# Four outputs instead of three in token halves behind each layer norm, one PSUM bank each

## The chip, the core and the metric

The kernel runs on one core of one Trainium2 chip, as one program that is launched once. The metric is the device time of that launch in microseconds (us); smaller is better. TensorE multiplies into PSUM, which has eight banks of 128 partitions and 512 fp32 values each; VectorE, ScalarE (ACT in the rows) and GpSimd (POOL) do the rest from SBUF, and SyncE (SP) issues the DMAs. In the rows PE stands for TensorE and DVE for VectorE.

## What is computed

One sequence of 512 tokens with 1024 features goes through two blocks, all in fp32. The first block has two layers, the second one:

```python
def first_block(x, c, ...):
    c_act = silu(c)
    for l in range(2):
        sh1, sc1, g1, sh2, sc2, g2 = split(c_act @ w_ada[l] + b_ada[l], 6)
        h = x * (1 + sc1) + sh1
        if l == 0:
            y = short_conv_mixer(h, ...)          # W_out(B * conv3(C * V))
        else:
            h_kv = x * (1 + kv_scale) + kv_shift  # shift and scale from c, too
            k, v = h_kv @ w_k, h_kv @ w_v         # 16 heads of 64
            F = cumsum(log_sigmoid(h_kv @ w_f + b_f))
            # causal softmax of q.k / 8 + F[t] - F[s], times v, times w_o
            y = forgetting_attention(h, w_q, k, v, F, w_o)
        x = layer_norm(alpha * x + g1 * y, ln1[l])
        h = x * (1 + sc2) + sh2
        y = (silu(h @ w_gate[l]) * (h @ w_up[l])) @ w_down[l]     # 2816 wide
        x = layer_norm(alpha * x + g2 * y, ln2[l])
    return x

def second_block(x, p, ...):
    z = rms_norm(x) @ w_in                        # 256+256+64+5*512 outputs
    a = mla(...)                                  # latent attention, 4 heads
    r = hgrn2(...)                                # gated linear attention, both directions
    x = x + concat(a, r) @ w_o
    x = x + swiglu(rms_norm(x))
    return x + sigmoid(rms_norm(x) @ w_ple_gate) * (p @ w_ple_proj)
```

## The kernel before

Activations lie transposed: 128 features on the partitions, the 512 tokens on the free axis, so a tensor of 1024 features is eight tiles. Each operand of a product is split into an upper part (names that end in h, `whi` for weights) and the remainder (l, `wlo`), and `mm3` adds upper by upper, upper by remainder and remainder by upper into the same PSUM bank. One output tile over 1024 features therefore takes 8 x 3 matmuls.

**Weights** are packed in units of eight blocks of 128 x 128, in the order in which the program asks for them. `_make_unit` loads a unit by DMA into one of three slots (raw), casts it on ACT (whi) and subtracts on VectorE, sometimes on GpSimd (wlo); there are four slots for whi and four for wlo. `weight` makes units up to one beyond the unit that is asked for. The raw slots are shared with the **adaptive modulation** (w_ada): `ada_pump` takes a column of it at a time and multiplies and sums it on VectorE (aj, ada).

**Order.** The code is recorded first. `plan` then lists every engine's instructions with a cost model, by the order in the program and by what each needs: tiles, SBUF slots and PSUM banks in three classes (g, s, o; at most 6, 5 and 4 of the eight). `issue` emits this list, so nearly all instructions have one source line, L573, and are told apart here by the names of their tiles.

**The four junctions.** After a layer norm the first outputs of the next product are made in two token halves of 256 columns: TensorE multiplies the A half of all eight tiles while VectorE still normalizes the B half. `out_halves` gives a half a bank of its own, A of class g and B of class s, so three outputs take six banks; each half is read out for itself. This happens at four places:

- first FFN, behind the convolution's layer norm (tiles hm0 to hm7): gate 0, up 0 and gate 1 (pg0, pu0, pg1) in halves, in `ffn`; up 1 (pu) follows at full width, then gate 2 (pg, called pg2 below);
- attention, behind the first FFN's layer norm (tiles hk): the forget gates (pf) and the first two key outputs (pk0, pk1) in `fox_block`; then the forget gates' path (zf, the cumulative sum F, a trip of F through memory, the probabilities Pa, Pm, Pb), keys, values (pv: two banks, each holding two tiles of 128 tokens for two outputs, in `fox_v`) and queries (pq, from tiles hq);
- second FFN, behind the attention's layer norm, through `ffn` again;
- second block, behind the second FFN's layer norm (tiles hx): three of the five latent outputs (cq0 to cq2) in `block2`; cq3 and cq4 and the gates (gt) follow at full width. Here the norm's factor (rx, rxr) comes last and is multiplied into the outputs; ACT copies the halves to SBUF (cl) before it is known.

`gemm` runs a group of outputs: half by half, in a half tile by tile, in a tile output by output. In the first FFN `ffn` calls `ada_pump` for three columns per feature f, starting at f = 0. At the end of the layer norm's B half, `ln_mid` scales the eight tiles of x for the residual (agln, abln).

## Time and profile before

| what | value |
|---|---|
| median of three runs | 1951.23 us (1949.99 to 1951.87) |
| the profiled execution's own time | 1948.55 us |
| its span, first to last instruction | 1946.8 us |
| mean granted TensorE clock | 0.989 |
| TensorE busy | 1897.0 us (97%) |
| VectorE busy | 1285.9 us (66%) |
| ACT, GpSimd busy | 819.9 us (42%), 191.5 us (10%) |
| chain that ended last | TensorE 84%, VectorE 11% |

The times in the profile are of that one execution, from the start of its span. A matmul's duration in a timeline includes its pipeline; how fast matmuls follow each other is read from their starts. "[1.29 <-ACT hm0h L573]" says that the engine stood still for 1.29 us ahead of this instruction, and that ACT's writing of hm0h ended that.

### The profile page before, as it was taken

How to read it: one execution, taken by the hardware profiler on the slowest of the kernel's cores; microseconds unless marked ns; L12 is line 12 of the kernel's file. 1: busy time of each engine (PE TensorE's matmuls, PEld its weight loads, DVE VectorE, ACT ScalarE, POOL GpSimd, SP SyncE). 2: the span in 40 equal slices, each digit the busy share in tenths (PEclk: the TensorE clock that was granted, in tenths of full speed). 3: DMA queues.
4: the chain of work that ended last, by engine and by line, in shares of the span. 5: the costliest groups of instructions: out<-in, count | busy, mean ns of one | idle time of the engine just before them, and what ended most of it. 6: DMA issues, size and time to landing. Idle time of an engine off the chain costs nothing.

```text
span 1946.8 us, 24436 instructions
## 1 busy us (share of the span) xinstructions
PE 1897.0 (97%) x9310; PEld 1589.9 (82%) x9310; DVE 1285.9 (66%) x2211; ACT 819.9 (42%) x1363; POOL 191.5 (10%) x150
## 2 busy tenths in 40 slices
PE   8999899999999899999999999999999999999998
PEld 7888788888888788888888888787877888888887
DVE  8877976564569898894523335999898654334445
ACT  5323432222346577553322233686684533223333
POOL 1000100000001322110000000122153000000000
PEclk9999999999999899999999999999998999999999
DMA  9674477674424222323322222322111222222242
GB/s 360 223 249 158 138 248 241 199 236 161 150 98 138 70 76 88 120 76 109 103 98 98 98 97 76 130 87 76 55 55 44 97 98 97 95 96 94 97 139 75
DMA packets 76470, 245.55 MB, mean 126 GB/s; under 512 B 8496, under 2 KB 9776, under 8 KB 76352
## 3 DMA queue, kind: packets, MB, share of 16 engines
q1 hardware_dynamic: 76352, 243.98, 37.7%
q8 instruction: 73, 1.20, 0.2%
q14 instruction: 45, 0.37, 0.1%
HBM read 235.53 MB, written 8.42 MB: 125 GB/s over the span
## 4 chain that ended last, share of the span: by engine, by line
PE 84%; DVE 11%; ACT 2%; issue 2%; DMA 1%; SPq 0%; DVEq 0%; ACTq 0%
PE pu L573 18%; PE pg L573 17%; PE pd L573 12%; PE ffn_down L573 5%; PE gt L573 4%; PE wo L573 2%; PE pl L573 2%; PE gb L573 2%; PE gc L573 2%; PE vv L573 2%; PE attn_o L573 1%; PE pq L573 1%; PE conv_out L573 1%; DVE wlo L573 1%; PE pv L573 1%
## 5 line engine op out<-in xcount | busy, mean ns | idle before, releaser
L573 ACT CAST whi<-raw 128x1024 fp32r<-128x1024 f32 (+1 forms) x313 | 326.2, 1043 | 625.9 <-PE pd L573 130.8
L573 DVE TENSOR_TENSOR wlo<-raw,whi 128x1024 fp32r<-128x1024 f32 (+1 forms) x286 | 353.5, 1237 | 324.4 <-ACT whi L573 320.6
L573 POOL TENSOR_TENSOR wlo<-raw,whi 128x1024 fp32r<-128x1024 f32 x27 | 65.6, 2429 | 1181.7 <-ACT whi L573 1181.7
L573 DVE CUSTOM_DVE_ANT_0 aj<-ada,cact,adab 128x1024 bf16<-128x1024 f32 x96 | 123.8, 1293 | 37.7 <-DMA ada<-in_wada 37.5
L573 DVE TENSOR_TENSOR s<-pu,s 128x512 f32<-128x512 f32 x42 | 29.0, 690 | 85.0 <-PE pu L573 85.0
L573 DVE TENSOR_TENSOR S<-S,sq 128x512 f32<-128x512 f32 (+1 forms) x62 | 36.7, 592 | 1.6 <-ACT sq L573 1.4
L573 ACT ACTIVATE s<-s 128x512 f32<-128x512 f32 x22 | 13.9, 632 | 54.0 <-DVE s L573 54.0
L573 ACT ACTIVATE s<-pg 128x512 f32<-128x512 f32 x40 | 23.6, 589 | 18.3 <-PE pg L573 18.3
L573 DVE CUSTOM_DVE_ANT_0 G<-S,G 128x128 f32<-128x128 f32 (+3 forms) x64 | 30.3, 484 | 0.5
L573 DVE TENSOR_TENSOR xr<-pd,xr 128x512 f32<-128x512 f32 x16 | 11.0, 690 | 26.9 <-PE pd L573 26.9
L573 DVE TENSOR_SCALAR G<-Fm,fneg 128x128 f32<-128x128 f32 x64 | 26.6, 419 | 0.4 <-PE po L573 0.2
L573 POOL TENSOR_TENSOR Fm<-Fb,cmask 128x512 f32<-128x512 f32 x14 | 18.6, 1336 | 63.9 <-DVE PT_2l L573 30.3
L573 ACT ACTIVATE sq<-axr 128x256 f32<-128x256 f32 (+1 forms) x33 | 15.1, 467 | 22.0 <-DVE axr L573 22.0
L573 DVE TENSOR_SCALAR G<-Fb,fneg 128x128 f32<-128x128 f32 (+2 forms) x48 | 23.0, 480 | 0.4 <-PE po L573 0.2
L573 DVE TENSOR_TENSOR s<-pg,rfr 128x512 f32<-128x512 f32 x22 | 15.2, 691 | 11.9 <-PE pg L573 11.9
L573 DVE TENSOR_TENSOR u<-pu,rfr 128x512 f32<-128x512 f32 x22 | 15.2, 691 | 11.7 <-PE pu L573 11.7
L573 PE MATMUL tp<-ident,Pa 128*128 128x128 f32 x64 | 16.7, 289 | 3.8 <-DVE Pa L573 3.8
L573 ACT ACTIVATE Pa<-G,negm 128x128 f32<-128x128 f32 (+1 forms) x32 | 16.2, 506 | 9.8 <-DVE negm L573 8.8
L573 ACT ACTIVATE sq<-x 128x256 f32<-128x256 f32 (+1 forms) x19 | 9.8, 517 | 22.2 <-DVE x L573 22.2
L573 PE MATMUL tp<-ident,Pb 128*128 128x128 f32 x64 | 16.8, 293 | 2.0 <-DVE Pb L573 1.9
L573 DVE TENSOR_TENSOR gz<-gt,rxr 128x512 f32<-128x512 f32 x20 | 13.6, 685 | 4.7 <-PE gt L573 4.7
L573 PE MATMUL pu<-hm2l,whi 128*128 128x512 f32 x42 | 16.4, 390 | 0.0
(4502 smaller groups left out, 6314.9 us busy)
## 6 DMA issues: line engine op xcount, KB each, us to landing
raw<-in_wpack SPq DMA_DIRECT2D x309, 512.0 KB, 3.5
ada<-in_wada SPq DMA_DIRECT2D x96, 512.0 KB, 4.2
ada<-in_wada SPq DMA_DIRECT2D x32, 256.0 KB, 6.0
Fb<-fd SPq DMA_DIRECT2D x16, 256.0 KB, 3.8
x<-in_xT SPq DMA_DIRECT2D x8, 256.0 KB, 6.0
pd<-pple SPq DMA_DIRECT2D x8, 256.0 KB, 6.2
xd<-x SPq DMA_DIRECT2D x8, 256.0 KB, 6.2
axr<-xd SPq DMA_DIRECT2D x8, 256.0 KB, 4.5
```

Of the source, the lines that this page charges most:

```text
L573: getattr(getattr(nc, op.unit), op.name)(*[get(x) for x in op.args], **{k: get(x) for k, x in op.kw.items()})
```

## The change

Class `Wide` keeps both halves of an output in one bank: the A half's sum is made in columns 0 to 255 and the B half's in 256 to 511, and the whole bank is read out once, behind the B half (`full`). `gemm_wide` runs such a group, and for its length sets `ahead` to 1, so that `weight` makes no unit ahead of the one asked for.

- In both FFNs four outputs run in halves (pg0, pu0, pg1, pu1), on four banks, and `ada_pump` isn't called for the first two features.
- In the attention the forget gates and two keys take three banks, and the first values are multiplied beside them (`values`, `fox_v_part`): per tile the values of the half's tokens come with the last key. The eight narrow copies of the forget gates' weights are made ahead of the group.
- In the second block cq0 to cq3 run in halves; they are multiplied by the norm's factor straight out of PSUM, and the ACT copies go.

```diff
--- before.py
+++ after.py
@@ -30,6 +30,8 @@
 B2_ORDER = """gate1 proj0 gate0 score0 prep0 proj1 score1 gate2 intra0 value0 value1 proj2 gate3 state0 gout0
 prep1 score2 intra1 state1 prep2 intra2 proj3 score3 value2 prep3 state2 gout1 intra3 state3
 gout3 value3 gout2"""
+EARLY = 4
+LATE = 4
 MIX_GROUPS = [(0, 1, 2), (3,), (4,), (5,), (6,), (7,)]
 SLOTS = 76
 RAWB = 3
@@ -576,13 +578,21 @@
             nc.scalar.preload_act_table_set(load_at[i])
 
 
+class Wide(list):
+
+
+    def __init__(self, ps):
+        super().__init__([(ps[:, :HT], slice(0, HT)), (ps[:, HT:], slice(HT, T))])
+        self.full = [(ps, slice(0, T))]
+
+
 class Build:
     def __init__(self, ctx, tc, aps):
         self.tc = tc
         self.nc = Recorder()
         self.a = aps
         self.blocks = []
-        self.n_units = 0
+        self.n_units, self.ahead = 0, 2
         self.unit = {}
         self.ada_next = 0
         self.ada_jobs = []
@@ -632,7 +642,7 @@
         i = len(self.blocks)
         self.blocks.append((wname, k, n))
         u, s = divmod(i, BLK)
-        while self.n_units < min(u + 2, NUNIT):
+        while self.n_units < min(u + self.ahead, NUNIT):
             self._make_unit(self.n_units)
             self.n_units += 1
         hi, lo = self.unit[u]
@@ -667,7 +677,10 @@
         return [(self.ps("g", name + "A")[:, :HT], slice(0, HT)),
                 (self.ps("s", name + "B")[:, :HT], slice(HT, T))]
 
-    def gemm(self, outs, acts, kouter=True):
+    def out_wide(self, name, tag="g"):
+        return Wide(self.ps(tag, name))
+
+    def gemm(self, outs, acts, kouter=True, also=None):
 
 
         nc = self.nc
@@ -679,8 +692,10 @@
             for i, o in order:
                 wname, n, pieces = o
                 k, xh, xl = acts[i]
+                if also is not None and o is outs[-1]:
+                    also(p, i, xh, xl)
                 if (i, n, wname) not in ws:
-                    ws[i, n, wname] = (self.side_by_side if wname == "w_f" else self.weight)(wname, k, n)
+                    ws[i, n, wname] = self.narrow[:, k, :] if wname == "w_f" else self.weight(wname, k, n)
                 ps, sl = pieces[p]
                 if wname == "w_f":
                     for j, x in enumerate((xh, xl)):
@@ -694,15 +709,19 @@
 
         nc = self.nc
         hi, lo = self.weight(wname, k, n)
-        if k == 0:
-            self.narrow = self.r("narrow", (P, ND, 64))
         t = self.narrow[:, k, :]
         nc.scalar.copy(t[:, :32], hi[:, :32])
         nc.scalar.copy(t[:, 32:], lo[:, 32:64])
         return t
 
-    def gemm_all(self, outs, acts, kouter=True):
-        for _ in self.gemm(outs, acts, kouter):
+    def gemm_wide(self, outs, acts, also=None):
+
+        self.ahead = 1
+        self.gemm_all(outs, acts, also=also)
+        self.ahead = 2
+
+    def gemm_all(self, outs, acts, kouter=True, also=None):
+        for _ in self.gemm(outs, acts, kouter, also):
             pass
 
 
@@ -1090,9 +1109,10 @@
         wg, wu, wd = names
         early = []
         if halves:
-            early = [(wg, 0, self.out_halves("pg0")), (wu, 0, self.out_halves("pu0")),
-                     (wg, 1, self.out_halves("pg1"))]
-            self.gemm_all(early, acts)
+            early = [(w, f, self.out_wide(f"p{w[4]}{f}", tag)) for f, tag in enumerate("gs"[:EARLY // 2])
+                     for w in (wg, wu)]
+            self.gemm_wide(early, acts)
+            early = [(w, f, o.full) for w, f, o in early]
         else:
             early = [(wg, 0, self.out("pg0")), (wu, 0, self.out("pu0")), (wg, 1, self.out("pg1"))]
             self.gemm_all(early, acts)
@@ -1110,7 +1130,8 @@
                     pc.append(made[w, f])
 
                 left = (len(self.ada_jobs) - (ND if wg == "ffn_gate0" else 0)) - self.ada_next
-                self.ada_pump(min(left, 3 if wg == "ffn_gate0" else 1))
+                if f >= len(early) // 2:
+                    self.ada_pump(min(left, 3 if wg == "ffn_gate0" else 1))
                 s = self.f(f"s{f}")
                 if rstd is None:
                     for ps, sl in pc[0]:
@@ -1213,8 +1234,20 @@
     def fox_block(self, kva, qa, rest, ln):
         nc = self.nc
         nc.group = "fox"
-        pf, *pk = (self.out_halves(n) for n in ("pf", "pk0", "pk1"))
-        self.gemm_all([("w_f", 0, pf), ("w_k", 0, pk[0]), ("w_k", 1, pk[1])], kva)
+        pf, *pk = (self.out_wide(n) for n in ("pf", "pk0", "pk1"))
+        pv = self.fox_v_banks(0, "s")
+        ws = {}
+
+        def values(p, i, xh, xl):
+            if p == 0:
+                ws[i] = self.weights("w_v", i, 0, VP)
+            self.fox_v_part(pv, p, i, xh, xl, ws[i])
+
+        self.narrow = self.r("narrow", (P, ND, 64))
+        for k in range(ND):
+            self.side_by_side("w_f", k, 0)
+        self.gemm_wide([("w_f", 0, pf), ("w_k", 0, pk[0]), ("w_k", 1, pk[1])], kva, also=values)
+        pf, *pk = (x.full for x in (pf, *pk))
         nc.group = "rest"
         rest()
         nc.group = "logf"
@@ -1236,7 +1269,7 @@
         nc.sync.dma_start(fd.all(), F)
 
         ks = [self.fox_k(f, kva, pk[f]) for f in range(2)]
-        vs = self.fox_v(0, kva)
+        vs = self.fox_v(0, kva, pv)
         q = [self.fox_q(0, qa)]
         tp = self.ps("s", "Ftp", (P, 4, H))
         for i in range(4):
@@ -1294,21 +1327,34 @@
             nc.scalar.copy(kb[top, sl], ps[bot])
         return ka, kb, kl
 
-    def fox_v(self, g, kva):
+    def fox_v_banks(self, g, tag="g"):
+        return [self.ps(tag, f"pv{g}_{i}", (P, 4 // VP, VP * P)) for i in range(VP)]
+
+    def fox_v_part(self, banks, p, k, xh, xl, w):
+
+        nc = self.nc
+        per = 4 // VP
+        wh, wl = w
+        for i in range(per):
+            j = p * per + i
+            tb = slice(j * P, (j + 1) * P)
+            out = banks[p][:, i, :]
+            nc.tensor.matmul(out, xh[:, tb], wh, start=(k == 0 and i == 0), stop=False)
+            nc.tensor.matmul(out, xh[:, tb], wl, start=False, stop=False)
+            nc.tensor.matmul(out, xl[:, tb], wh, start=False, stop=(k == 7 and i == per - 1))
+
+    def fox_v(self, g, kva, banks=None):
 
 
         nc = self.nc
         nc.group = f"v{g}"
         per = 4 // VP
-        banks = [self.ps("g", f"pv{g}_{i}", (P, per, VP * P)) for i in range(VP)]
-        for k, xh, xl in kva:
-            wh, wl = self.weights("w_v", k, g * VP, VP)
-            for j in range(4):
-                tb = slice(j * P, (j + 1) * P)
-                out = banks[j // per][:, j % per, :]
-                nc.tensor.matmul(out, xh[:, tb], wh, start=(k == 0 and j % per == 0), stop=False)
-                nc.tensor.matmul(out, xh[:, tb], wl, start=False, stop=False)
-                nc.tensor.matmul(out, xl[:, tb], wh, start=False, stop=(k == 7 and j % per == per - 1))
+        if banks is None:
+            banks = self.fox_v_banks(g)
+            for k, xh, xl in kva:
+                w = self.weights("w_v", k, g * VP, VP)
+                for p in range(VP):
+                    self.fox_v_part(banks, p, k, xh, xl, w)
         v = []
         for c in range(VP):
             f = g * VP + c
@@ -1482,21 +1528,17 @@
         nc = self.nc
         nc.group = "lat"
 
-        c0 = [self.out_halves(f"cq{i}") for i in range(3)]
-        self.gemm_all([("w_in", i, c0[i]) for i in range(3)], acts)
+        c0 = [self.out_wide(f"cq{i}", "ggggs"[i]) for i in range(LATE)]
+        self.gemm_wide([("w_in", i, c0[i]) for i in range(LATE)], acts)
+        c0 = [x.full for x in c0]
         rx = res["rx"]
         cs = []
         for i in range(5):
-            if i >= 3:
+            if i >= LATE:
                 c0.append(self.out(f"cq{i}"))
                 self.gemm_all([("w_in", i, c0[i])], acts)
             t = self.f(f"cl{i}")
-            if i < 3:
-                for ps, sl in c0[i]:
-                    nc.scalar.copy(t[:, sl], ps)
-                nc.vector.tensor_tensor(t, t, rx, ALU.mult)
-            else:
-                nc.vector.tensor_tensor(t, c0[i][0][0], rx, ALU.mult)
+            nc.vector.tensor_tensor(t, c0[i][0][0], rx, ALU.mult)
             cs.append(t)
         xd = self.dram("xd2", (ND, P, T))
         for f in range(ND):
```

On VectorE, in the first FFN junction, the B half of the layer norm (x, conv_outmu and conv_outrstd are the residual and its statistics, hm..e the scaled tile, the ISA rows the modulation sums). Before:

```order
L573 TENSOR_SCALAR hm01e<-x_125,m0G,m0B 128x256
L573 ISA aj_2023,ada<-ada_1873,cact,adab 128x1024
L573 ISA ada 128x1
L573 TENSOR_TENSOR hm0l<-hm01e,hm0h 128x256
L573 TENSOR_TENSOR x_197<-x_197,conv_outmu_1856 128x256
L573 ISA aj_2041,ada<-ada_1877,cact,adab 128x1024
L573 ISA ada 128x1
L573 TENSOR_TENSOR x_197<-x_197,conv_outrstd 128x256
L573 TENSOR_TENSOR x_235<-x_235,conv_outmu_1856 128x256
L573 TENSOR_SCALAR hm11e<-x_197,m0G,m0B 128x256
L573 TENSOR_TENSOR x_235<-x_235,conv_outrstd 128x256
L573 TENSOR_TENSOR hm1l<-hm11e,hm1h 128x256
```

The same piece with the change:

```order
L575 TENSOR_SCALAR hm01e<-x_123,m0G,m0B 128x256
L575 TENSOR_TENSOR x_195<-x_195,conv_outrstd 128x256
L575 TENSOR_TENSOR hm0l<-hm01e,hm0h 128x256
L575 TENSOR_SCALAR hm11e<-x_195,m0G,m0B 128x256
L575 TENSOR_TENSOR x_235<-x_235,conv_outmu_1856 128x256
L575 TENSOR_TENSOR hm1l<-hm11e,hm1h 128x256
```

The modulation sums between the tiles are gone from this piece (a third stood ahead of hm01e); they now come behind the first two hidden features.

On VectorE at the end of the same half, with the weight remainders of the units that follow. Before, a remainder stood between tiles 4 and 5, and the end read:

```order
L573 TENSOR_SCALAR x_125<-x_125,agln_292,abln_294 128x512
L573 TENSOR_SCALAR hm71e<-x_499,m0G,m0B 128x256
L573 TENSOR_SCALAR x_197<-x_197,agln_292,abln_294 128x512
L573 TENSOR_TENSOR hm7l<-hm71e,hm7h 128x256
L573 ISA aj_2164,ada<-ada_2037,cact,adab 128x1024
```

With the change:

```order
L575 TENSOR_TENSOR hm7l<-hm71e,hm7h 128x256
L575 TENSOR_SCALAR x_235<-x_235,agln_292,abln_294 128x512
L575 TENSOR_SCALAR x_280<-x_280,agln_292,abln_294 128x512
L575 TENSOR_SCALAR x_347<-x_347,agln_292,abln_294 128x512
L575 TENSOR_SCALAR x_402<-x_402,agln_292,abln_294 128x512
L575 TENSOR_SCALAR x_447<-x_447,agln_292,abln_294 128x512
L575 TENSOR_SCALAR x_499<-x_499,agln_292,abln_294 128x512
L575 TENSOR_TENSOR wlo_2176<-raw_1871,whi_2100 128x1024
L575 TENSOR_TENSOR wlo_2187<-raw_1873,whi_2138 128x1024
```

All eight scalings now stand ahead of the next unit's remainder, two before hm7l and six behind it.

On TensorE in the attention, where the first probabilities are transposed (tp) and the second pair of value banks (pv_0, pv_1) is summed. Before:

```order
L573 MATMUL pv_0_5467<-whi_5328,hk7l 128x256
L573 MATMUL tp_0_5556<-ident,Pa_5379 128x128
L573 MATMUL tp_0_5556<-ident,Pm_5393 128x128
L573 MATMUL tp_0_5556<-ident,Pa_5379 128x128
L573 MATMUL tp_0_5556<-ident,Pb_5500 128x128
```

With the change:

```order
L575 MATMUL pv_0_5453<-wlo_5338,hk5h 128x256
L575 MATMUL tp_0_5567<-ident,Pa_5402 128x128
L575 MATMUL pv_0_5453<-whi_5320,hk5l 128x256
L575 MATMUL pv_1_5466<-whi_5320,hk5h 128x256
L575 MATMUL pv_1_5466<-wlo_5338,hk5h 128x256
L575 MATMUL pv_1_5466<-whi_5320,hk5l 128x256
```

Before, one bank was complete ahead of the transposes and the other came after them; now both have come to tile 5 when the first transpose is due.

## Rows read from the trace of the kernel before

**Rows 1.** Page, busy time of each engine, share of the span, instructions.

```profile
PE 1897.0 (97%) x9310; PEld 1589.9 (82%) x9310; DVE 1285.9 (66%) x2211; ACT 819.9 (42%) x1363; POOL 191.5 (10%) x150
```

**Rows 2.** Windows, all stretches: busy us (count) by engine, granted clock, DMA.

```profile
198.00:233.00 35.00, 28.00 (x179) 23.36 (x178) 34.54 (x87) 16.24 (x29) 4.23 (x5) 1.00 0.33 106
850.00:880.00 30.00, 27.52 (x179) 24.24 (x180) 29.07 (x76) 17.68 (x32) 1.23 (x2) 1.00 0.20 68
608.00:616.00 8.00, 6.24 (x16) 4.94 (x17) 7.94 (x23) 3.88 (x8) 1.27 (x1) 0.57 0.09 34
640.00:704.00 64.00, 54.01 (x294) 43.91 (x294) 54.35 (x142) 39.35 (x97) 19.87 (x15) 0.92 0.19 65
704.00:788.00 84.00, 84.00 (x523) 75.25 (x522) 74.62 (x207) 58.43 (x144) 22.95 (x13) 1.00 0.30 101
1218.00:1238.00 20.00, 16.97 (x96) 13.68 (x95) 19.88 (x54) 11.81 (x30) 3.48 (x2) 0.91 0.25 87
1280.00:1480.00 200.00, 191.82 (x971) 156.36 (x970) 185.36 (x312) 143.32 (x258) 60.07 (x43) 0.96 0.19 64
```

**Rows 3.** Chain of what ended last, by time: start, us, instructions.

```profile
182.89 2.88 PE conv_out6A L573 x24
...
233.03 5.44 PE pg L573 x24
```

**Rows 4.** Timeline of TensorE, first FFN: start, us, operation, [idle <-releaser].

```profile
202.42 0.39 PE L573 MATMUL pg0A<-hm0h,whi 128*128 128x256 f32 x1 [1.29 <-ACT hm0h L573]
...
204.20 0.39 PE L573 MATMUL pg0A<-hm0l,whi 128*128 128x256 f32 x1 [1.17 <-DVE hm0l L573]
...
213.80 0.28 PE L573 MATMUL pg1A<-hm7h,wlo 128*128 128x256 f32 x1
...
216.18 0.39 PE L573 MATMUL pg0B<-hm0l,whi 128*128 128x256 f32 x1 [1.51 <-DVE hm0l L573]
...
218.69 0.39 PE L573 MATMUL pg0B<-hm1h,whi 128*128 128x256 f32 x1 [1.06 <-ACT hm1h L573]
...
232.87 0.39 PE L573 MATMUL pg<-hm0h,whi 128*128 128x512 f32 x1
```

**Rows 5.** Timeline of VectorE, first FFN junction, second half.

```profile
212.98 1.27 DVE L573 CUSTOM_DVE_ANT_0 aj<-ada,cact,adab 128x1024 bf16<-128x1024 f32 x1
...
215.71 0.42 DVE L573 TENSOR_TENSOR hm0l<-hm01e,hm0h 128x256 fp32r<-128x256 f32 x1
...
223.57 1.23 DVE L573 TENSOR_TENSOR wlo<-raw,whi 128x1024 fp32r<-128x1024 f32 x1
...
227.03 0.55 DVE L573 TENSOR_SCALAR x<-x,agln,abln 128x512 f32<-128x512 f32 x1
...
228.26 0.42 DVE L573 TENSOR_TENSOR hm7l<-hm71e,hm7h 128x256 fp32r<-128x256 f32 x1
```

**Rows 6.** Timelines of TensorE and VectorE, second FFN junction.

```profile
864.73 0.28 PE L573 MATMUL pg1A<-hm7h,wlo 128*128 128x256 f32 x1
...
879.50 0.39 PE L573 MATMUL pg<-hm0h,whi 128*128 128x512 f32 x1
...
877.29 2.83 DVE L573 TENSOR_SCALAR axr<-axr,agln,abln 128x512 f32<-128x512 f32 x6
```

**Rows 7.** Timeline of TensorE, start of the attention.

```profile
609.76 0.77 PE L573 MATMUL pq<-hq0h,whi 128*128 128x512 f32 x1 [3.84 <-DVE zf L573]
...
617.82 0.39 PE L573 MATMUL pq<-hq7h,wlo 128*128 128x512 f32 x1
...
646.48 0.33 PE L573 MATMUL tp<-ident,Pa 128*128 128x128 f32 x1 [1.62 <-DVE Pa L573]
```

**Rows 8.** Timelines of VectorE and TensorE, second block's start.

```profile
1249.45 0.48 DVE L573 SCALAR_TENSOR_TENSOR hx7l<-axr,vec,hx7h 128x256 fp32r<-128x256 f32 x1
...
1256.81 0.39 PE L573 MATMUL gt<-hx0h,whi 128*128 128x512 f32 x1
...
1259.10 1.89 DVE L573 TENSOR_TENSOR cl<-cl,rxr 128x512 f32<-128x512 f32 x3
```

## The prediction

> **What bounds the kernel now.** I read the page first. TensorE is busy 97% of the span [rows 1], so the whole kernel holds about 50 us in which it stands still. I then looked for these 50 us by stretch. Behind the attention's start TensorE is busy for all of 84 us [rows 2]: time won ahead of such a stretch stays won, if the engine has more work ready. It stands still in front of that, at the four places where a layer norm meets the next product: 7.0 us between 198 and 233 (first FFN), 2.5 us between 850 and 880 (second FFN), 10.0 us between 640 and 704 (attention), 3.0 us between 1218 and 1238 (second block) [rows 2]. VectorE is busy 34.5 of the 35 us of the first [rows 2]. So a junction is a race: VectorE makes the normalized halves tile by tile, TensorE eats them.
>
> The price of a matmul comes from the chain by time: 24 of 256 columns take 2.88 us, 24 of 512 take 5.44 us [rows 3], so 0.120 and 0.227 us each. An output in two halves costs 48 x 0.120 = 5.76 us, 0.32 more than in one piece. A tile's half feeds 9 matmuls (1.08 us) with three outputs and 12 (1.44 us) with four.
>
> **First FFN junction.** The A half runs from 202.42 to 213.92: 72 matmuls, 8.64 us of work and 2.86 us of waits, the largest 1.17 us for hm0l [rows 4]. With four outputs there are 11.52 us of work. Eight instead of six matmuls stand ahead of hm0l, so some 0.9 us of its wait stays; every later tile comes before TensorE is through with the one ahead. A ends at about 202.42 + 11.52 + 0.9 = 214.8, only 0.9 us later than now, with 24 more matmuls done.
>
> The B half is where the change tells. Now VectorE runs three adaptive-modulation sums (aj; one row stands for them) of 1.27 us ahead of the second tile, and later a weight remainder (wlo) of 1.23 us; TensorE waits 1.51 us for hm0l and 1.06 us for hm1h and comes to the next gate output (pg2) at 232.87 [rows 4, 5]. The order of after has neither aj nor wlo in that piece, because the pump is not called for the first two features and no unit is made ahead. From 212.98 to the end of hm7l at 228.68 are 15.7 us [rows 5]; less three aj (3.8), one wlo (1.2) and two scalings agln (1.1) 9.6 us remain, 1.2 us a tile, less than TensorE's 1.44. So B is bound by TensorE: 214.8 + 11.5 = 226.3. Now pg2 needs its wlo, which stands behind eight agln in the order of after: hm7l at 212.98 + 9.6 + 1.1 = 223.7, six agln of 0.47 (2.83 for six [rows 6]) to 226.5, wlo to 227.7. I let pg2 start at 227.5, since its first matmul needs no remainder: **5.4 us won**. Bounds: 6.5 without that wait, 4.1 if a second wlo is in it. The aj that were moved land in stretches where VectorE, busy 66% of the span [rows 1], has room.
>
> **Second FFN junction.** The same with no aj in it. A ends at 864.85 and pg2 starts at 879.50 [rows 6]. The 24 extra matmuls (2.9 us) go mostly into the 2.5 us of idle time of this window [rows 2]; A ends at about 865.7, B at 877.2. But wlo is again behind the agln. The last six of these start at 877.29 now [rows 6], with two wlo of 1.23 us in the B half ahead of them; without these two they run from 874.8 to 877.6, and pg2's wlo ends at 878.9. Products of two upper halves need no wlo and can go ahead of it, so I take 878.0, between the two ends: **1.5 us**, with bounds of 0.5 (wlo in full) and 2.5 (all of the idle time).
>
> **Attention.** Now six halves and two banks of values take all eight PSUM banks, and the first query product waits 3.84 us, until zf is read out of pf; its 24 matmuls then run from 609.76 to 618.05, 8.3 us where 5.4 is normal, at a granted clock of 0.57 in 608 to 616 [rows 2, 7], that is partly at the lower of the two levels (1.2 and 2.4 GHz). After, pf, two keys and two values take five banks, so the queries can follow at once: 3.84 + 2.85 = 6.7 us at that place. (The Trainium skill, "TensorE: Matmul & The Clock Gate", in the section on a second failure mode of the clock by cycling through PSUM, tells of just such pauses between matmul groups that let the clock fall; this row agrees, and by that rule 2.85 of the 6.7 us is clock.) How much of it stays? The path of the forget gates (zf, scan, a trip through memory, probabilities Pa) isn't shortened: the first transposes wait for Pa at 646.48 [rows 7]. Between 640 and 704 neither TensorE (54.0 of 64 us) nor VectorE (54.4) is full [rows 2]; the work done early, which is the second values bank (48 matmuls, 5.76 us), is missed there only where TensorE was the one waited for. VectorE is at 85% there. I keep **3.0 us**, about half. Bounds: all 6.7; or a loss of 2.9, where the pause moves to the wait for Pa and as many products as here run at the lower clock a second time.
>
> Half A of an output cannot be read while half B is summed in the same bank. (The Trainium skill, "PSUM — Partial Sum Buffer", section on bank collisions, wants two engines kept off one bank at a time; it speaks against the change, since the four outputs' evacuation no longer overlaps the B half. No run here shows a collision.) That costs nothing where nobody waits: zf is made shortly before 609.76, and the products of this block end 3.84 us ahead of that [rows 7], so VectorE comes to pf later than TensorE is done with it.
>
> **Second block.** Here VectorE is full (19.9 of 20 us, 1218 to 1238 [rows 2]) and bounds the A half; 24 more matmuls fit into the 3.0 us of idle time. B is filled with other outputs already. Won: 2.88 less 2 x 0.32 is 2.2 us at most, plus six ACT copies that go. But in the mixing part, 1280 to 1480, TensorE is busy 191.8 and VectorE 185.4 of 200 us [rows 2], and a part of it will be lost there. I take **1.5 us**, between 2.6 and a loss of 2.
>
> **Sum.** 5.4 + 1.5 + 3.0 + 1.5 = 11.4 us off the profiled execution's 1948.55 us, that is 1937.2. That execution is 2.7 us below the median of 1951.23, so on the median's scale 1939.8: I say **1940**.
>
> **The rivals.** *FFN junctions alone.* Attention and mixing are bound by their own chains of VectorE and transfers, and whatever TensorE does ahead is waited away. For it: the wait for Pa and 85% of VectorE; against it: 10.0 us of idle TensorE in 640 to 704 and the full stretch behind it [rows 2, 7]. 5.4 + 1.5 off: 1944.3.
> *Everything kept.* 6.5 + 2.5 + 6.7 + 2.6 = 18.3 off: 1933. Against it: wlo behind the agln in the order.
> *Slower: weights come late.* The wide block holds all four weight slots until B leaves each, and unit makers run one less ahead. If each junction then stands w longer than in my sum, the time is 1940 + 4w. It decides from w = 2.8 on; with six agln (2.83) and two wlo (2.46) behind the end of B at every junction, w = 5.3, 1961. Against it: B takes 11.5 us, and the first unit's slot is free after its first two tiles, so that the cast lies well ahead.
> *Nothing changes.* Now too, 512-wide matmuls of the fourth output stand among those of B, so the planner fills the waits anyway and the change only trades fillers; at three junctions it pays 0.32 us: 1952. For it, the second FFN junction, where B shows hardly an idle moment; against it, 7.0 us of idle time at the first.
> *PSUM in the second block.* cq0 to cq3 are now held until the norm's factor multiplies them out, at 1259.10; the gates start at 1256.81 and want the next bank 5.4 us later [rows 8]. They would have to come 3.1 us earlier to wait. hx7l is ready at 1249.45 [rows 8], and I expect 2: it costs nothing then, and is counted in the loss bound.
>
> **How the numbers follow.** Forecast 0.48, FFN alone 0.24, everything 0.10, late weights 0.07, no change 0.11. About 0.2% (3.9 us) is what a measurement of this kernel can tell from no change. Faster by more: 0.48 + 0.24 + 0.10 = 0.82; same 0.11; slower 0.07. The range from 1934 to 1948 holds the forecast with its bounds and the first rival; it leaves out late weights, no change and the far end of the second.
>
> **What would show it.** Right: aj gone from VectorE between hm0l and hm7l; no idle time over 0.5 us in the first B half; pg2 near 227.5 after the same start; the first query matmul within 1 us of the last of the block, at full clock; the first transposes near 641, that is 646.48 less the first FFN's gain and no more. Wrong: pg2 waiting for wlo for over 2 us; a long TensorE pause ahead of the transposes; a mixing part that is longer than before.

## The result and the profile after

The changed kernel takes 1940.29 us (median of four runs, 1938.51 to 1942.59), the kernel before 1950.9 us beside it: a ratio of 0.9946, 95% interval 0.9932 to 0.996, 10.6 us less. The profiled execution's span went from 1946.8 to 1937.8 us. First its page, busy time by engine:

```profile
PE 1893.9 (98%) x9382; PEld 1593.3 (82%) x9382; DVE 1284.3 (66%) x2208; ACT 817.4 (42%) x1344; POOL 190.3 (10%) x148
```

TensorE's busy time fell by 3.1 us [rows 1], the span by 9.0; the other 5.9 us are idle time that is gone. The same stretches as in [rows 2], from the windows of after (busy us and count of TensorE, its weight loads, VectorE, ACT, GpSimd, then granted clock and DMA):

```profile
198.00:233.00 35.00, 31.56 (x232) 28.98 (x231) 34.41 (x86) 19.35 (x32) 4.23 (x5) 1.00 0.18 63
850.00:880.00 30.00, 29.27 (x207) 27.09 (x206) 28.37 (x70) 16.33 (x25) 0.00 (x0) 1.00 0.16 54
640.00:704.00 64.00, 56.22 (x273) 44.89 (x273) 52.42 (x153) 36.89 (x93) 20.46 (x15) 0.87 0.17 58
704.00:788.00 84.00, 82.27 (x508) 71.90 (x507) 76.91 (x201) 59.92 (x148) 26.44 (x14) 1.00 0.34 113
```

These windows are fixed times, while the work in them has moved, so they show where the engine still waits, not what was won: 3.4 us idle in place of 7.0 at the first FFN, 0.7 in place of 2.5 at the second, 7.8 in place of 10.0 in the attention, at a lower clock, and 1.7 us of new idle time in the 84 us behind it that had none.

What was won is read from products that both kernels share: the last of one stretch and the first of the next. From the timeline of TensorE, before:

```profile
197.87 0.28 PE L573 MATMUL conv_out7B<-y7h,wlo 128*128 128x256 f32 x1
...
330.79 0.39 PE L573 MATMUL pd<-hid0h,whi 128*128 128x512 f32 x1
...
571.76 0.28 PE L573 MATMUL ffn_down07B<-hid21h,wlo 128*128 128x256 f32 x1
...
792.46 0.48 PE L573 MATMUL attn_o<-o0h,whi 128*128 128x512 f32 x1
...
849.29 0.28 PE L573 MATMUL attn_o7B<-o7h,wlo 128*128 128x256 f32 x1
...
977.42 0.39 PE L573 MATMUL pd<-hid0h,whi 128*128 128x512 f32 x1
...
1218.39 0.28 PE L573 MATMUL ffn_down17B<-hid21h,wlo 128*128 128x256 f32 x1
...
1285.91 0.60 PE L573 MATMUL gvt<-ident,gz 128*128 128x128 f32 x4
...
1537.72 0.39 PE L573 MATMUL pg<-hf0h,whi 128*128 128x512 f32 x1
...
1941.66 0.28 PE L573 MATMUL pl7B<-hg7h,wlo 128*128 128x256 f32 x1
```

and after:

```profile
199.21 0.28 PE L575 MATMUL conv_out7B<-y7h,wlo 128*128 128x256 f32 x1
...
326.82 0.39 PE L575 MATMUL pd<-hid0h,whi 128*128 128x512 f32 x1
...
567.78 0.28 PE L575 MATMUL ffn_down07B<-hid21h,wlo 128*128 128x256 f32 x1
...
786.52 0.48 PE L575 MATMUL attn_o<-o0h,whi 128*128 128x512 f32 x1
...
843.35 0.28 PE L575 MATMUL attn_o7B<-o7h,wlo 128*128 128x256 f32 x1
...
969.85 0.39 PE L575 MATMUL pd<-hid0h,whi 128*128 128x512 f32 x1
...
1210.82 0.28 PE L575 MATMUL ffn_down17B<-hid21h,wlo 128*128 128x256 f32 x1
...
1276.81 0.60 PE L575 MATMUL gvt<-ident,gz 128*128 128x128 f32 x4
...
1529.04 0.39 PE L575 MATMUL pg<-hf0h,whi 128*128 128x512 f32 x1
...
1932.78 0.28 PE L575 MATMUL pl7B<-hg7h,wlo 128*128 128x256 f32 x1
```

Differences of these rows give the stretches:

| stretch | before | after | won | forecast |
|---|---|---|---|---|
| start to last conv_out product | 197.87 | 199.21 | -1.34 | 0 |
| to the first down product (first FFN) | 132.92 | 127.61 | 5.31 | 5.4 |
| from the last ffn_down0 to the first attn_o product (attention) | 220.70 | 218.74 | 1.96 | 3.0 |
| from the last attn_o to the first down product (second FFN) | 128.13 | 126.50 | 1.63 | 1.5 |
| from the last ffn_down1 to the first gvt product (second block's start) | 67.52 | 65.99 | 1.53 | 1.5 less what mixing gives back |
| from there to the last FFN's first gate (mixing) | 251.81 | 252.23 | -0.42 | |

All else differs by 0.2 us in all. A stretch here is what one profiled execution of each kernel shows; how far such a stretch varies without any edit is taken up with the experiments. The first row belongs to no edit: with the same code ahead of it, that point lay between 197.6 and 200.9 us in the kernels below.

The first junction in detail, TensorE after (1.34 us are to be taken off for the scale of before):

```profile
203.76 0.39 PE L575 MATMUL pg<-hm0h,whi 128*128 128x256 f32 x1 [1.29 <-ACT hm0h L575]
...
205.54 0.38 PE L575 MATMUL pg<-hm0l,whi 128*128 128x256 f32 x1 [1.04 <-DVE hm0l L575]
...
228.28 0.40 PE L575 MATMUL pg<-hm0h,whi 128*128 128x512 f32 x1
...
229.22 0.50 PE L575 MATMUL pg<-hm0h,wlo 128*128 128x512 f32 x1 [0.30 <-DVE wlo L575]
```

and VectorE:

```profile
215.32 0.41 DVE L575 TENSOR_TENSOR hm0l<-hm01e,hm0h 128x256 fp32r<-128x256 f32 x1
...
224.88 0.41 DVE L575 TENSOR_TENSOR hm7l<-hm71e,hm7h 128x256 fp32r<-128x256 f32 x1
...
225.21 2.82 DVE L575 TENSOR_SCALAR x<-x,agln,abln 128x512 f32<-128x512 f32 x6
...
227.95 2.35 DVE L575 TENSOR_TENSOR wlo<-raw,whi 128x1024 fp32r<-128x1024 f32 x2
```

hm0l of the B half follows hm7l of the A half with no sums between, VectorE is through at 225.2, and from 205.54 on TensorE stands still only for the 0.30 us in which the remainder wlo ends, behind the six scalings. pg2 starts at 228.28, 226.94 on the scale of before. That is 5.9 us sooner than the 232.87 of before [rows 4]; 0.6 of it is lost again at wlo, so that 5.3 arrive at the first down product.

At the second junction the wait for hm3h, before and then after, and the start of pg2 after:

```profile
858.08 0.39 PE L573 MATMUL pg0A<-hm3h,whi 128*128 128x256 f32 x1 [1.02 <-ACT hm3h L573]
```

```profile
852.14 0.39 PE L575 MATMUL pg<-hm3h,whi 128*128 128x256 f32 x1 [0.42 <-ACT hm3h L575]
...
871.26 0.40 PE L575 MATMUL pg<-hm0h,whi 128*128 128x512 f32 x1
```

The other waits in its A half were 1.00 us for hm0l and 0.31 for hm1l; after, 0.89 for hm0l is left. On the scale of before (5.94 us later) pg2 comes at 877.20 in place of 879.50 [rows 6], and 0.7 of these 2.3 us are lost again behind it, where TensorE waits 0.30 us for wlo.

In the attention, the second query output's start before, and TensorE after:

```profile
618.49 0.51 PE L573 MATMUL pq<-hq0h,whi 128*128 128x512 f32 x1
```

```profile
600.13 0.40 PE L575 MATMUL pq<-hq0h,whi 128*128 128x512 f32 x1
...
605.60 0.39 PE L575 MATMUL pq<-hq0h,whi 128*128 128x512 f32 x1
...
610.03 0.42 PE L575 MATMUL Ftp<-ident,F 16*128 16x16 f32 x4 [2.46 <-DVE F L575]
...
638.62 0.30 PE L575 MATMUL tp<-ident,Pa 128*128 128x128 f32 x1 [0.76 <-DVE Pa L575]
```

From the last product of ffn_down0 to the second query output's start it is 37.8 us, where it was 46.7; to the first transpose 70.8, where it was 74.7 [rows 7]; to attn_o 218.7, where it was 220.7. The lead of 8.9 us shrinks at every step. The wait for zf is gone, and a wait of 2.46 us for F stands in its place; the query products behind it follow each other every 0.43 us at first, where 0.23 is the rate ahead of the wait, and the granted clock in 608 to 616 is 0.79.

### The profile page after: what moved, and what is told of

Its sections match the earlier page's. It is cut to its first block, busy times and chain, and to the rows that moved or that the text cites. A ratio compares the mean times of both kernels' runs of the same rounds, so it can differ in the third digit from the quotient of the medians.

```text
span 1937.8 us, 24555 instructions
## 1 busy us (share of the span) xinstructions
PE 1893.9 (98%) x9382; PEld 1593.3 (82%) x9382; DVE 1284.3 (66%) x2208; ACT 817.4 (42%) x1344; POOL 190.3 (10%) x148
## 4 chain that ended last, share of the span: by engine, by line
PE 57%; DVE 7%; ACT 2%; issue 1%; DVEq 0%; ACTq 0%
PE pu L575 12%; PE pg L575 12%; PE pd L575 9%; PE gt L575 4%; PE ffn_down L575 2%; PE wo L575 2%; PE pl L575 2%; PE attn_o L575 1%; DVE axr L575 1%; PE pv L575 1%; PE po L575 1%; PE pq L575 1%; PE MS L575 1%; PE tp L575 1%; PE pk L575 1%; PE S L575 1%
## 5 line engine op out<-in xcount | busy, mean ns | idle before, releaser
L575 PE MATMUL pg<-hm0l,whi 128*128 128x512 f32 (+1 forms) x48 | 18.0, 376 | 1.9 <-DVE hm0l L575 1.9
L575 PE MATMUL pg<-hm0h,whi 128*128 128x512 f32 (+1 forms) x48 | 18.0, 378 | 1.3 <-ACT hm0h L575 1.3
L575 PE MATMUL pg<-hm0h,wlo 128*128 128x512 f32 (+1 forms) x48 | 18.0, 376 | 0.6 <-DVE wlo L575 0.6
```

The source lines that it names most:

```text
L575: getattr(getattr(nc, op.unit), op.name)(*[get(x) for x in op.args], **{k: get(x) for k, x in op.kw.items()})
```

## The experiments

Each has its profile, so that the stretches of the table can be compared; times are medians beside runs of the kernel before on the same chip.

**The modulation sums alone** (kernel before, three outputs in halves):

```diff
-                self.ada_pump(min(left, 3 if wg == "ffn_gate0" else 1))
+                if f >= 2 or not halves:
+                    self.ada_pump(min(left, 3 if wg == "ffn_gate0" else 1))
```

> The kernel before, with one part of the change: no modulation sums are asked for at the first two features of the FFNs that run in halves; three outputs in halves on six banks as before. Theory A (the junction is a race, and VectorE's three sums in the B half were what TensorE mostly waited for): VectorE ends the B half at about 224, TensorE has 8.6 us of halves and 5.4 us of pu from 213.9 on, so pg2 comes at 228 to 228.5 on the scale of before instead of 232.87: 4.4 to 4.9 us won at this junction, time 1946 to 1946.5. Rival B (it is the fourth output in halves that wins, and the sums only fill time that is idle anyway): under 1 us, time 1950 to 1951.

1945.41 us, ratio 0.9976 (0.9967 to 0.9984). The first FFN's stretch is 4.00 us shorter, the second FFN's and the second block's start the same to 0.01. TensorE's timeline:

```profile
215.34 0.39 PE L573 MATMUL pg0B<-hm0l,whi 128*128 128x256 f32 x1 [0.24 <-DVE hm0l L573]
...
229.76 0.39 PE L573 MATMUL pg<-hm0h,whi 128*128 128x512 f32 x1
```

The wait for hm0l of the B half is 0.24 us in place of 1.51. Theory A holds, with 4.0 us where it had 4.4 to 4.9; three quarters of the first junction's 5.3 us come with the sums alone. The attention, whose code is that of before, took 2.5 us longer here, and mixing 2.2 us less: this is taken up below.

**The sums back in the changed kernel.**

```diff
-                if f >= len(early) // 2:
+                if True:
```

> The changed kernel, with the modulation sums back at the first two features; all else as changed. Theory A: the three sums (3.8 us) stand again in the B half or just behind it, VectorE ends it at about 227.5 on the scale of before and the weight remainder follows, so of the first FFN's 5.3 us 1.4 to 2.5 stay: 1943 to 1944. Rival B: nearly all of it stays, 1940 to 1941.

1960.97 us, ratio 1.0056 (1.0043 to 1.0068). Both theories fall: the first FFN's stretch is 7.4 us longer than before. TensorE, VectorE and SyncE's DMA queue (a row of the queue is a run of issues, so many of them):

```profile
237.83 0.80 PE L575 MATMUL pg<-hm0h,whi 128*128 128x512 f32 x1 [9.59 <-ACT whi L575]
```

```profile
226.33 1.28 DVE L575 CUSTOM_DVE_ANT_0 aj<-ada,cact,adab 128x1024 bf16<-128x1024 f32 x1
...
237.81 1.23 DVE L575 TENSOR_TENSOR wlo<-raw,whi 128x1024 fp32r<-128x1024 f32 x1 [1.57 <-ACT whi L575]
```

```profile
194.88 35.51 SPq L575 DMA_DIRECT2D ada<-in_wada  x6
...
233.25 3.34 SPq L575 DMA_DIRECT2D raw<-in_wpack  x3
```

The sums cost the B half no VectorE time: the planner put them behind the scalings, at 226.3. But their columns are loaded ahead of the wide block and hold the raw slots all that time, and three more columns stand in SyncE's queue ahead of the next weights. So the queue stands still until 227.65, when the first sum (226.33) has freed a slot, the unit for pg2 is issued at 233.25, and TensorE waits 9.59 us for its cast. That is the slower rival of the prediction, brought about by one line. The kernel before bears the same columns, with its sums at 212.98 and on [rows 5] and a unit made ahead; that the missing unit ahead is what makes the columns harmful is likely, but no run tests it by itself.

**A fourth raw slot, sums back.**

```diff
-SLOTS = 76
-RAWB = 3
+SLOTS = 74
+RAWB = 4
@@
-                if f >= len(early) // 2:
+                if True:
```

> The changed kernel with the modulation sums back at the first two features, as in the run that lost 7.4 us at the first FFN, but with four raw slots instead of three (and 74 instead of 76 general slots). Theory G (there the sums' columns took the raw slots while the wide block held all four weight slots, so that the next unit's DMA was issued too late): the wait of 9.6 us for whi shrinks to under 4, the first FFN's stretch comes to within 3 us of before. Rival B2 (VectorE's time for the sums is what was lost): it stays at 7 us over before.

One run, 1968.25 us, and 7.2 us longer than before at the first FFN. The DMA queue and TensorE:

```profile
201.75 28.26 SPq L575 DMA_DIRECT2D ada<-in_wada  x3
...
230.88 3.94 SPq L575 DMA_DIRECT2D raw<-in_wpack  x3
```

```profile
237.44 0.79 PE L575 MATMUL pg<-hm0h,whi 128*128 128x512 f32 x1 [8.15 <-ACT whi L575]
```

Theory G falls as it was put: one slot more doesn't help. It goes to another column, and the weights are again behind the queue's wait, 28 us for one run of columns. What remains of theory G is the order in the queue, which is read from these rows and not tested by a run that changes it; B2 gave the right number, but TensorE's wait is for the cast of the late weights and not for VectorE.

**Banks only** (sums away, the same three outputs in both FFNs, both halves in one bank).

```diff
-            early = [(wg, 0, self.out_halves("pg0")), (wu, 0, self.out_halves("pu0")),
-                     (wg, 1, self.out_halves("pg1"))]
+            early = [(wg, 0, self.out_wide("pg0")), (wu, 0, self.out_wide("pu0")),
+                     (wg, 1, self.out_wide("pg1", "s"))]
             self.gemm_all(early, acts)
+            early = [(w, f, o.full) for w, f, o in early]
...
```

> The kernel before without modulation sums for the first two features, and in both FFNs the same three outputs in halves, but both halves of an output in one bank. It differs from the run with the sums alone taken away in the banks only. Theory A (banks are not what the FFN junctions wait for; the extra work in the A half is): 4.0 us at the first FFN as in that run, nothing at the second. Rival F (one bank instead of two, with one reading out, is what wins at the second): 1.6 us at the second FFN.

1947.84 us, ratio 0.9989 (0.9979 to 0.9998). First FFN 3.75 us won (with a granted clock of 0.64 in 206 to 210), second 0.21. Theory A holds, F falls: in the FFNs the one bank wins next to nothing by itself; it makes room for the fourth output. The rest, 5.3 - 4.0 = 1.3 us at the first and 1.6 at the second junction, comes with the fourth output and with `ahead` at 1 together: here `ahead` is still 2, and no run parts these two.

**The FFNs' part alone.** Attention and second block are those of before. The diff is seen from the changed kernel and shows a part of the edit:

```diff
-        c0 = [self.out_wide(f"cq{i}", "ggggs"[i]) for i in range(LATE)]
-        self.gemm_wide([("w_in", i, c0[i]) for i in range(LATE)], acts)
+        c0 = [self.out_halves(f"cq{i}") for i in range(3)]
+        self.gemm_all([("w_in", i, c0[i]) for i in range(3)], acts)
...
-        self.gemm_wide([("w_f", 0, pf), ("w_k", 0, pk[0]), ("w_k", 1, pk[1])], kva, also=values)
+        self.gemm_all([("w_f", 0, pf), ("w_k", 0, pk[0]), ("w_k", 1, pk[1])], kva)
...
```

> The kernel before with the two FFNs' part of the change alone: four outputs in halves and no modulation sums for the first two features; attention and second block as before. Theory A: 5.3 us at the first FFN and 1.6 us at the second, as in the changed kernel, no gain at the second block; with an attention as before 1943 to 1944. Rival E as for the run of the attention alone: the same two gains, and the attention's stretch, whose code is that of before, changes its length by up to 2.5 us either way with the planner's list.

1946.1 us, ratio 0.9979 (0.9969 to 0.9988). Second FFN 1.68 us won, second block's start 0.0, attention 0.2, and mixing 4.6 us lost with its code unchanged. The first FFN won 3.27 us, not 5.3; its windows from 202 on differ from those of the run with only the attention put back (5.27 us won), which has the same products in the same order there, mainly in the clock and so in the products done. First that run, then this one:

```profile
202.00:206.00 4.00, 2.56 (x19) 2.36 (x20) 3.64 (x10) 3.94 (x8) 2.61 (x5) 1.00 0.40 131
206.00:210.00 4.00, 4.00 (x34) 3.95 (x34) 4.00 (x14) 1.61 (x3) 0.00 (x0) 1.00 0.00 0
```

```profile
202.00:206.00 4.00, 2.58 (x12) 2.38 (x13) 3.64 (x10) 3.94 (x8) 2.59 (x5) 0.69 0.39 131
206.00:210.00 4.00, 4.00 (x21) 4.00 (x20) 4.00 (x14) 1.58 (x3) 0.00 (x0) 0.50 0.00 0
```

The clock, the last number but two, is 0.69 and then 0.50, that is the lower level of 1.2 GHz, in the first tiles of the A half, behind the same wait for hm0h and hm0l.

**The second block's part undone.**

```diff
-        c0 = [self.out_wide(f"cq{i}", "ggggs"[i]) for i in range(LATE)]
-        self.gemm_wide([("w_in", i, c0[i]) for i in range(LATE)], acts)
-        c0 = [x.full for x in c0]
+        c0 = [self.out_halves(f"cq{i}") for i in range(3)]
+        self.gemm_all([("w_in", i, c0[i]) for i in range(3)], acts)
...
```

> The changed kernel with the second block's first outputs as before (three in halves on six banks, copied by ScalarE). Theory A: the 1.7 us that the change wins between the second FFN's last product and the first gvt product are gone, and so is the 0.6 us that the mixing part gives back: 1941 to 1942. Rival D (they are won by the clock, which is higher in the A half with the change, and not by the work moved): the same time, but the granted clock there is back at about 0.9.

1940.86 us, ratio 0.9958 (0.9944 to 0.9972). The second block's start is as long as before to 0.02 us, and mixing is 0.2 us shorter than before: the 1.5 us are this part's. The difference to the changed kernel is too small for the times. Rival D isn't borne out: in the run of the FFNs' part alone the block's start is as long as before to 0.02 us at a granted clock of 1.00 from 1209 to 1234.

**The attention's part**, undone in the changed kernel, and then alone in the kernel before.

```diff
-        pf, *pk = (self.out_wide(n) for n in ("pf", "pk0", "pk1"))
-        pv = self.fox_v_banks(0, "s")
+        pf, *pk = (self.out_halves(n) for n in ("pf", "pk0", "pk1"))
...
-        vs = self.fox_v(0, kva, pv)
+        vs = self.fox_v(0, kva)
...
```

> The changed kernel with the attention's start as before (forget gates and two keys in halves on six banks, values behind them). Theory A: the attention's stretch (first product of the forget gates to first product of attn_o) takes 2.0 us longer than in the changed kernel, with the wait of 3.8 us for zf back, and the time is 1942. Rival C (the attention is bound by its own chain and the 2.0 us are the order's luck elsewhere): the stretch differs by under 0.5 us, 1940.

1943.56 us, ratio 0.9962 (0.995 to 0.9975). The time is what theory A said, the stretch isn't: without the part it is 2.4 us *shorter* than before, so no longer than with it, though the wait of 3.84 us for zf is back. What this kernel's profile has over that of the changed kernel lies in mixing (3.1 us longer than before), which the edit doesn't touch.

> The kernel before with the attention's part of the change alone: forget gates and two keys on one bank each, first values beside them; FFNs and second block as before. Theory A (part of the lead that TensorE has at the queries is kept): the stretch from the FFN's last product to attn_o is 2 to 3 us shorter than before, 1947 to 1948. Rival E (the lead is waited away in the forget gates' chain, and the stretch's length goes with the order in which the planner happens to list the probabilities): the queries come 8 to 9 us sooner, but the stretch ends anywhere from 2.5 us earlier to 5 us later, as in the runs so far that had this part (-2.0, -1.8, +5.4) or had it not (0, +2.5, -2.4).

The part alone: 1950.87 us, ratio 1.0002 (0.9993 to 1.0012). TensorE:

```profile
608.69 0.40 PE L575 MATMUL pq<-hq0h,whi 128*128 128x512 f32 x1
...
616.59 0.42 PE L575 MATMUL Ftp<-ident,F 16*128 16x16 f32 x4 [0.92 <-DVE F L575]
...
649.59 0.27 PE L575 MATMUL tp<-ident,Pa 128*128 128x128 f32 x1
```

The last ffn_down0 product is at 575.01 here, so the queries start after 33.7 us, where it was 38.0 before, with no wait for zf ahead of them; the first transpose comes after 74.6 us, where it was 74.7, and the stretch is 0.8 us longer in the end. The lead is gone here before the first probability is used. Theory A falls. Rival E holds for the stretch; its queries come 4.3 us sooner at the first output and 7.6 at the second (39.1 us in place of 46.7), not 8 to 9.

**The same work in another order.** Both kernels, with one constant of the planner's cost model changed, and so another list wherever two instructions are nearly equal:

```diff
-            return 13.4 + max(size / 2.4, 95) if dt == F32R else 3 + size / 2.4
+            return 13.6 + max(size / 2.4, 95) if dt == F32R else 3 + size / 2.4
```

> The changed kernel with one constant of the planner's cost model for a matmul at 13.6 ns instead of 13.4: the same work, another list in the attention behind the first transposes and in the mixing part. Theory A: gains at the four junctions as in the changed kernel, attention included (-2 within 0.5), time within 2 us of 1940. Rival E: the first two and the last junction keep theirs, the attention and the mixing part differ by 1 to 4 us.

> The kernel before with the same constant at 13.6: no part of the change. Theory A: junctions and time as before within 1 us. Rival E: junctions as before, attention and mixing part differ by 1 to 4 us from the kernel before, either way.

> The changed kernel with the planner's constant for a matmul at 13.2 ns instead of 13.4: another list for the same work. Rival E by now the favoured one: first FFN -5.3 (or up to 2 us less where the clock is low in the A half), second FFN -1.65, second block -1.5 to -2; the attention's stretch anywhere from -2.5 to +2.5 against before. Theory A: attention -2 within 0.5.

> The kernel before with the same constant at 13.2 ns. Rival E: junctions as before, the attention's stretch anywhere from -2.5 to +2.5 us. Theory A: within 0.5 us of before.

With 13.6: changed kernel 1945.73 us, ratio 0.9975 (0.9964 to 0.9985), kernel before 1952.97, ratio 1.0017 (1.0008 to 1.0027). With 13.2, one run each: 1942.02 and 1955.37. The stretches against the kernel before, all runs together (us, minus is shorter; the last run has two general slots less, so its attention and mixing are not compared with the rest):

| kernel | first FFN | attention | second FFN | second block's start | mixing |
|---|---|---|---|---|---|
| changed | -5.3 | -2.0 | -1.6 | -1.5 | +0.4 |
| changed, 13.6 | -5.3 | +1.9 | -1.7 | -2.0 | +3.8 |
| changed, 13.2 | -5.3 | -2.7 | -1.7 | -2.1 | +5.0 |
| changed, attention undone | -5.3 | -2.4 | -1.7 | -1.6 | +3.1 |
| changed, second block undone | -4.5 | -1.8 | -1.7 | 0.0 | -0.2 |
| before, with the FFNs' part | -3.3 | -0.2 | -1.7 | 0.0 | +4.6 |
| before, with the attention's part | +0.3 | +0.8 | +0.3 | 0.0 | -2.6 |
| before, without the sums | -4.0 | +2.5 | 0.0 | 0.0 | -2.2 |
| before, without the sums, three on one bank each | -3.8 | 0.0 | -0.2 | 0.0 | +2.3 |
| before, 13.6 | +0.3 | -1.4 | 0.0 | 0.0 | +4.0 |
| before, 13.2 | 0.0 | -2.8 | 0.0 | 0.0 | +7.2 |
| changed, sums back | +7.4 | +5.4 | -1.5 | -1.5 | +2.2 |
| changed, sums back, fourth raw slot | +7.2 | -6.5 | -1.6 | -2.1 | +18.5 |

The two stretches vary as rival E has it, and more: the attention with its code as before is anywhere from 2.8 us shorter to 2.5 us longer, with the new code from 2.7 us shorter to 5.4 longer, and mixing, whose code no kernel changes, from 2.6 us shorter to 7.2 longer. The cause that rival E names, the planner's list, is shown only in part. The runs without the sums and with three on one bank each have the same order of instructions on TensorE, VectorE, ACT and GpSimd through the whole attention (507 on VectorE, 347 on ACT), and their stretches still lie 2.5 us apart. From the first query product to the second output's it took 8.70 us in the one (606.99 to 615.69) and 7.62 in the other (606.90 to 614.52), behind a wait of 3.7 us for zf in both, and the clock differs. First the run without the sums, then the other:

```profile
606.00:614.00 8.00, 7.01 (x19) 5.56 (x20) 7.94 (x21) 3.88 (x8) 1.27 (x1) 0.58 0.15 50
```

```profile
606.00:614.00 8.00, 7.10 (x24) 5.57 (x24) 7.94 (x21) 3.88 (x8) 1.28 (x1) 0.79 0.16 55
```

In mixing, the runs without the sums and with the second block undone have the same order and lie 2.0 us apart. So one and the same order took 2.0 and 2.5 us longer in one kernel's execution than in another's, and with one profile of each kernel the list's own share can't be told in the attention; in mixing the spread of 9.7 us is several times as large. The junctions of the FFNs and of the second block answer to their edits, within 0.3 us at the FFNs (the clock at the first left aside) and 0.6 at the second block.

## Why the prediction came out right

**The sum.** 1940 was forecast, 1940.29 measured, on the likeliest case. That it fits to 0.3 us is luck. The sum took 11.4 us off the profiled execution, and the profiled executions differ by 9.0 (1948.55 and 1939.52): 1.0 us less came in the attention, 0.4 was lost in mixing and 1.3 in the start that no edit touches. Most of this was made up for by the step to the median: the profiled execution lay 2.7 us below it before, and 0.8 after. 5.3 + 1.6 + 1.5 = 8.5 us at the two FFNs and the second block are shown by taking parts away or adding them alone. No run ties the attention's 2.0 us, the mixing's 0.4 or the starts to an edit.

**The first FFN** (5.4 forecast, 5.3 measured) went as worked out: sums out of the B half, B bound by TensorE, pg2 behind B. On the scale of before wlo came at 227.9, as worked out (227.7), behind the scalings; B ended 0.6 us later than worked out (226.9 in place of 226.3), and the first two products of pg2 need no wlo, so the wait that I had put at 1.2 us cost 0.6, of which 0.3 is idle time. The two misses cancel. The prediction didn't say how the gain divides: 4.0 us belong to the sums, 1.3 to the fourth output with `ahead` at 1.

**The second FFN and the second block** (1.5 and 1.5 forecast, 1.6 and 1.5 measured) hold as mechanisms too. At the second FFN A and B ended where they were worked out to end (865.7 and 877.2 on the scale of before), and wlo was waited for as expected. In the second block TensorE waited about 0.22 us for each of hx4 to hx7 in the A half before, and for none of them after; against that its first product there comes 0.8 us later, behind a new wait of 1.26 us for S. The forecast of 1.5 was meant with mixing's loss taken off; mixing was 0.4 us longer, which would leave 1.1, but this is less than that stretch varies with the same list.

**The attention** is where a step failed though its size fits the range: "the work done early ... is missed there only where TensorE was the one waited for", of which I kept about half. The first half of the step is right and was too small: at the second query output TensorE is 8.9 us ahead, against 6.7 worked out, because the block ends 1.8 us sooner, too; the first query output runs at full clock (24 products in 5.47 us, from 600.13 to 605.60). But the wait for F and the lower clock behind it take more than half of the lead back: the transposes of F come only 4.1 us sooner. The loss bound had the pause move to the wait for Pa; it moved to F. And in all kernels that have the part, nothing of this lead can be told at attn_o from what another list, or another execution of the same list, does to the same work. The first transposes, which were to come sooner by the first FFN's gain and no more, came at 638.62, 7.9 us sooner, of which 4.0 are the first FFN's gain less the later start; with the part alone they came 0.1 us sooner, counted from the last ffn_down0 product. So that expectation failed too, and a lead does get that far in some kernels: in the four that have the part and the sums out of the way the first transposes come 70.5 to 72.3 us behind that product, in the seven without the part 74.0 to 76.1; from there to attn_o it then takes 147.5 to 150.3 us with the part and 143.1 to 147.1 without. That the part wins nothing at all isn't shown either: six profiles with it average +0.3 us and seven without it -0.6, each group scattered over more than 5 us (the run with a fourth raw slot left aside). Where the lead goes behind the transposes stays open.

**The rivals.** "FFN junctions alone" names what is shown of the mechanism better than the forecast does, though the second block keeps its gain. "Late weights" didn't come, but the run with the sums back shows how near it was: a wait of 9.59 us at one junction, more than the 5.3 at which it was priced. "Nothing changes" falls with the 1.6 us at the second FFN, where it had its best case. "PSUM in the second block": the gates waited for no bank.

## What to carry to other kernels

Where a list scheduler orders the work, read what an edit wins from stretches between products that both kernels share, and set it against a neutral new list and against another profile of the same list: here a cost constant changed by 0.2 ns moved stretches that nothing touched by up to 7 us, more than the largest gain, and the same order gave stretches 2.5 us apart. Before a block that holds all slots of a buffer, look at what stands in the DMA queue ahead of its next load, not only at the engines; work that no one needs soon is best kept out of that queue. And a lead of the busiest engine at one point is not yet time won: here 8.9 us of it at the queries were 2.0 at the next shared product, no more than that stretch varies by itself.

## What the hardware showed that I had not expected

- The clock at the start of the A half of the first FFN differs between executions of the same instructions behind the same waits (about 3 us of them). With four outputs in halves and the sums away the granted clock from 206 to 210 is 1.00 in four kernels and 0.71 and 0.50 in two; these two win 0.8 and 2.0 us less of the 5.3. With three outputs, where TensorE waits for VectorE in this half anyway, it is 1.00 in three kernels and 0.57, 0.63 and 0.64 in three others, whose stretches are 0.3 us longer at most.
- The first 198 us, the same code in every kernel, ended between 197.6 and 200.9 us.
- Reading 512 columns at once in place of two times 256, with the first half held in PSUM for the whole second half, cost next to nothing at the two FFNs, where it was tried by itself: 0.21 us won at the second, 0.25 lost at the first, where the clock was at 0.64. By the Trainium skill, "Perfetto Trace Analysis", section "Matmuls", groups should rotate through banks so that reading one overlaps the next; here, where nobody waits for these outputs, no gain of the rotation is seen, and holding all eight banks went with the wait of 3.84 us in front of the queries [rows 7], which is gone with five banks and back when the attention's part is undone.
